# Token gathers of a mixture-of-experts layer: 128 indices each, with the unneeded ones past the table's end

## The chip, the cores and the metric

The kernel runs on one core of a Trainium2 chip. The metric is device time of one execution in microseconds (us), the median of several. Engines are named as in the profile: PE (TensorE matmuls; PEld its weight loads), DVE (VectorE), ACT (ScalarE), POOL (GpSimd), SP (SyncE, which here only issues DMAs). All DMAs, whoever issues them, are carried by 16 DMA engines. Queue q1 of the profile holds the DMAs that SP issues, q0 those that POOL issues.

## The reference

One decoder layer on 512 tokens of width 1024, in float32. What matters here is its last part, the expert layer on `x1` (the tokens after attention and the first normalisation):

```python
logits = (xf @ w_router + b_router)            # 32 experts
top_vals, top_idx = lax.top_k(logits, 4)       # each token goes to 4 experts
gates = softmax(top_vals)
...
xb = x_pad[rows]                               # the rows of one expert's tokens
g = min(xb @ w_gate[e] + b_gate[e], 7)
u = clip(xb @ w_up[e] + b_up[e], -7, 7)
h = g * sigmoid(1.702 * g) * (u + 1)
y = h @ w_down[e] + b_down[e]                  # added to its tokens, times the gate
```

Each expert has three weight matrices of 1024x1024 float32, 4 MiB each, so the 32 experts read 96 matrices. 512 x 4 = 2048 rows go to experts in all.

## The kernel before

Attention, output projection, first normalisation and router take roughly the first 300 us. The expert layer follows, in 32 steps of one expert each. Steps 0, 1 and every odd step up to 29 are *large* (96 token slots), the even steps from 2 to 28 and the last two are *small* (64 slots). Experts are ranked by their number of tokens, so large steps take those with many. With the reference's inputs the router gives these numbers of tokens (counted from the reference's own router):

| steps | tokens in the order of the steps |
|---|---|
| small, 2 to 28 | 64 63 62 62 60 59 59 59 58 57 56 50 50 48 (sum 807) |
| large, 3 to 29 | 89 83 80 73 73 72 70 70 68 67 67 67 67 64 (sum 1010) |
| 0, 1, 30, 31 | 74, 70, 48, 39 |

**Weights.** SP issues them in a fixed order by `wload` (line 669), each matrix as two DMAs of 2 MiB, into a ring of eight 2 MiB tiles with one further tile now and then. An issue waits until PE has finished with the tile that it overwrites.

**Rows of a step.** Two or three steps ahead, `route_info` (or `route_tokens` for step 1) multiplies a one-hot matrix with token numbers on PE, and DVE makes from it `ix` (the token number of each slot, one slot a partition; 0 where a slot has no token) and `gt` (its gate; 0 where a slot has no token). Column 0 holds slots 0 to 63 (twice over the partitions), column 1 slots 64 to 95 (four times). `gather` (line 975) turns `ix` into integers `ii` on 64 partitions, for a large step on 32 more (lines 977 and 979), and POOL issues an indirect DMA (line 981) that reads row `ii[p]` of `x1d` in HBM into partition p of the tile `xg`: 64 or 96 rows of 4 KB. Empty slots fetch row 0. `load_x` (lines 1031 to 1040) then transposes `xg` on PE into `xgA` or `xgB` for the matmuls; there is one buffer of `xg`, so a gather waits until the transposes of the step before have read it. The first step (`gather_early`, line 864) and the last two (`route_pair`, line 1027, 128 rows for two small steps) have gathers of their own.

**Rows back.** `store` (lines 1152 to 1157) computes indices on DVE, and POOL issues indirect DMAs that add the result rows onto `accd` in HBM: one a small step, two a large one, 128 indices each.

**The tile's first user.** Before any of these gathers, the tile `xg` serves as `bds`: `bdown_load` (line 945) has SP read the 32 rows of `b_down` into its first 32 partitions (line 947), and ACT and DVE make `bd3` from it (`bdown_prep`, lines 951 to 953).

Of the kernel before, what the change touches and what calls it, by code (L numbers as in the profile page):

```python
# [9 lines left out]
F32 = mybir.dt.float32  # L10
# [4 lines left out]
ALU = mybir.AluOpType  # L15
# [4 lines left out]
P = 128  # L20
T = 512
NT = T // P
D = 1024
KD = D // P
E = 32
# [20 lines left out]
def _const_array():  # L46
    cols = []

    def put(name, a):
        a = np.asarray(a, np.float32)  # L50
        off = sum(c.shape[1] for c in cols)
        _C[name] = (off, a.shape[1])
        cols.append(a)

    p = np.arange(P)
    put("ident", np.eye(P))
    put("iota", np.tile(np.arange(T)[None, :], (P, 1)))
    ia = (500000.0 ** (-np.arange(0, 32, 2) / 32.0)).astype(np.float32)
    ib = (500000.0 ** (-np.arange(0, 16, 2) / 16.0)).astype(np.float32)
    put("invrow", np.tile(np.concatenate([ia, ib])[None, :], (P, 1)))  # L60
    put("invT", (np.where(p % 32 < 16, -1.0, 1.0) * ia[p % 16])[:, None])
    tb = np.zeros((P, 2 * NT), np.float32)
    tb[:, :NT] = p[:, None]
    tb[:, NT:] = (np.arange(NT) * P)[None, :]
    put("tokid", tb)
    key = (E - 1 - np.arange(E)).astype(np.float32)
    for i in range(NFIX):
        key[i] += 200000.0 + 50000.0 * (NFIX - i)
    put("keyrow", np.tile(key[None, :], (P, 1)))
    put("keycol", key[p % E][:, None])  # L70
    put("eid", (p % E)[:, None])
    seq = np.asarray(RANK_OF_STEP, np.float32)
    sb = np.full((P, 2 * E), -1.0, np.float32)
    sb[96:128, 0:E] = seq
    sb[0:32, E:] = seq
    sb[64:96, E:] = seq
    put("seqblk", sb)
    put("seqrow", np.tile(seq[None, :], (P, 1)))
    put("iodup", np.tile(np.concatenate([np.arange(64)] * 2 + [np.arange(64, 96)] * 4)[None, :], (P, 1)))
    pad = np.stack([T + p % 64, T + 64 + p % 32], 1)  # L80
    put("padrow", pad)
    put("padidx", np.stack([2 * pad[:, 0] + p // 64, 4 * pad[:, 1] + p // 32], 1))
    put("rowmul", np.tile(np.array([[2.0, 4.0]]), (P, 1)))
    put("j64", np.tile((64.0 * np.arange(8))[None, :], (P, 1)))
    return np.ascontiguousarray(np.concatenate(cols, 1))


CONST = _const_array()


# [12 lines left out]
def kernel(ctx: ExitStack, tc: tile.TileContext, a: dict, out: bass.AP, dbg=None):  # L103
    nc = tc.nc
    dbg = dbg or {}
    V, S, G, PE = nc.vector, nc.scalar, nc.gpsimd, nc.tensor
# [9 lines left out]
    x1d = dr.tile([T, D], F32, name="x1d")  # L116
# [21 lines left out]
    def C(name):  # L138
        o, n = _C[name]
        return cst[:, o:o + n]  # L140
# [34 lines left out]
    def bank(name):  # L175
        return pp.tile([P, 512], F32, tag="b", name=name)
# [765 lines left out]
    p3 = ctx.enter_context(tc.tile_pool(name="p3", bufs=1))  # L942
    xgB = p3.tile([P, KD, 96], F32, name="xgB")
    bd3 = p3.tile([96, D], F32R, name="bd3")
    def bdown_load():
        b = p3.tile([P, D], F32, tag="xg", name="bds")[0:E]
        nc.sync.dma_start(b, a["b_down"])
        return b

# [12 lines left out]
    def route_tiles(n):  # L962
        xs = p3.tile([P, 2, 8], F32, tag="xs", name=f"xs{n}", bufs=3)
        ix = p3.tile([P, 2], F32, tag="ix", name=f"ix{n}", bufs=4)
        gt = p3.tile([P, 2], F32, tag="gt", name=f"gt{n}", bufs=4)
        ii = p3.tile([P, 1], I32, tag="ii", name=f"ii{n}", bufs=3)
        return xs, ix, gt, ii

    def route_mm(px, oh, rhs_t, large, lo, hi):
        for c in range(2 if large else 1):  # L970
            for t in range(NT):
                PE.matmul(px[:, 8 * c + lo:8 * c + hi], oh[:, t, 128 * c:128 * c + 128], rhs_t(t),
                          start=(t == 0), stop=(t == NT - 1))

    def gather(n, ii, ix, large):
        Cn = 96 if large else 64
        V.tensor_copy(ii[0:64], ix[0:64, 0:1])  # L977
        if large:
            V.tensor_copy(ii[64:96], ix[64:96, 1:2])
        xg = p3.tile([P, D], F32, tag="xg", name=f"xg{n}")  # L980
        G.indirect_dma_start(out=xg[0:Cn], out_offset=None, in_=x1d,  # L981
                             in_offset=bass.IndirectOffsetOnAxis(ap=ii[0:Cn], axis=0))
        return xg

    def route_info(n, oh, rhs_t, large):
        px = ps_tr(f"px{n}").rearrange("p a b -> p (a b)")
        route_mm(px, oh, rhs_t, large, 0, 5)
        nx = 2 if large else 1
        xs, ix, gt, ii = route_tiles(n)
        V.tensor_copy(xs[:, 0:nx, 0:5], px[:, 0:16].rearrange("p (a b) -> p a b", a=2)[:, 0:nx, 0:5])  # L990
        V.tensor_tensor(ix[:, 0:nx], xs[:, 0:nx, 0], xs[:, 0:nx, 1], ALU.add)
        V.tensor_reduce(gt[:, 0:nx], xs[:, 0:nx, 2:5], AX.X, ALU.add)
        return ii, ix, gt

    def route_tokens(n, oh):
        px = bank(f"pxt{n}")
        route_mm(px, oh, lambda t: RT[:, t, 0:2, n], True, 0, 2)
        xs, ix, gt, ii = route_tiles(n)
        V.tensor_copy(xs[:, :, 0:2], px[:, 0:16].rearrange("p (a b) -> p a b", a=2)[:, :, 0:2])
        V.tensor_tensor(ix, xs[:, :, 0], xs[:, :, 1], ALU.add)  # L1000
        return xs, gather(n, ii, ix, True), ix, gt

    def route_gates(n, oh, xs, xg, ix, gt):
        px = bank(f"pxw{n}")
# [4 lines left out]

    def route(n, oh, rhs_t, large):  # L1010
        ii, ix, gt = route_info(n, oh, rhs_t, large)
        return gather(n, ii, ix, large), ix, gt

    def route_pair(n, oh):
        px = bank(f"px{n}")
# [181 lines left out]
    def overflow(nv):  # L1197
# [45 lines left out]
        with tc.For_i(0, nv, 1) as i:  # L1243
# [15 lines left out]
            V.tensor_tensor(gr_, gr_, rt[:, :, 3], ALU.subtract)  # L1259
            V.tensor_copy(rt[:, :, 4], gr_)  # L1260
            xg, ix, gt = route(100, route_oh(100, row[:, 0:NT].unsqueeze(2), False), lambda t: rt[:, t, :], False)
            xt = load_x(100, xg, False)
            pg_ = ps_gu("ovpg")
# [40 lines left out]
    def rstep(s, oh):  # L1304
        return route(s, oh, lambda t: RT[:, t, :, s], LARGE[s])

    bds = bdown_load()

    scr = xgB.rearrange("p a b -> p (a b)")
# [301 lines left out]
    mat64(pu_, xgA, st0.wu, sel0, b3[:, 1, :], ks=range(1, 2))  # L1611
    bdown_prep(bds)
    rt1 = route_tokens(1, oh1)
    g, sg = swi_g1(0, pg0, 512)
    prep_counts()
# [97 lines left out]
```

## Time and profile before

| | |
|---|---|
| three runs | 1352.81, 1354.06, 1355.06 us; median 1354.06 us |
| the profiled execution | 1354.38 us, of which the span from first to last instruction is 1352.6 us |
| busy in the span | PE 92%, DVE 29%, ACT 19%, POOL 13% |
| moved by DMA | 454.28 MB; q1 428.15 MB, q0 24.78 MB |

Shares of busy time are averages over the whole span. The DMA share of a stretch is the time that its packets took, over 16 engines and the stretch's length; packets of one engine can overlap, so it can be a little over 1. The chain of waits follows, from the last instruction back, what released each piece of work; a "DMA" piece in it lasts from the DMA's issue to its landing, the time in the DMA queue included.

### The profile page before, as it was taken

The page shows a single profiled execution, that of the slowest core. Times are in us where ns is not written, and L with a number is a line of the kernel's source. Part 1 is how long each engine was busy: PE and PEld are TensorE (multiplying, and loading weights), DVE is VectorE, ACT ScalarE, POOL GpSimd, SP SyncE. Part 2 cuts the span into 40 slices and gives each one's busy share as a digit, 9 for nine tenths or more (in the row PEclk, how much of TensorE's full clock was granted, in tenths as well). Part 3 has the DMA queues.
Part 4 walks back from the last instruction along what each step waited for, and adds up shares of the span by engine and source line. Part 5 has one row for each costly group of instructions (what it writes and reads, how often), then busy time and mean ns, then how long its engine had stood idle before and what let it go on. Part 6 is the DMA issues. An engine that isn't in the chain of part 4 may idle for free.

```text
span 1352.6 us, 20619 instructions
## 1 busy us (share of the span) xinstructions
PE 1240.9 (92%) x8596; PEld 577.6 (43%) x8596; DVE 392.3 (29%) x1020; ACT 262.7 (19%) x588; POOL 179.0 (13%) x184
## 2 busy tenths in 40 slices
PE   9999998898999999898989898989797989899985
PEld 8887555443344343333333333333333333333331
DVE  6765667453121211111111111111111111111125
ACT  5544655231101111011101010101010101010113
POOL 0540221001011011011010101010101010100013
PEclk9999999898999999999999999999999999899978
DMA  8031064489999999999999999999999999999992
GB/s 312 0 125 63 7 256 171 172 333 358 380 390 401 394 381 403 395 401 394 403 396 402 394 399 399 398 398 400 397 398 396 402 394 401 397 420 409 420 377 97
DMA packets 45824, 454.28 MB, mean 336 GB/s; under 512 B 5856, under 2 KB 8672, under 8 KB 20256
## 3 DMA queue, kind: packets, MB, share of 16 engines
q1 hardware_dynamic: 34848, 428.15, 78.3%
q0 software_dynamic: 10880, 24.78, 7.4%
q8 instruction: 69, 1.13, 0.3%
q14 instruction: 27, 0.22, 0.0%
HBM read 436.39 MB, written 16.52 MB: 335 GB/s over the span
## 4 chain that ended last, share of the span: by engine, by line
PE 57%; DMA 38%; DVE 2%; issue 1%; ACT 0%; SPq 0%; POOL 0%; POOLq 0%; DVEq 0%; ACTq 0%
DMA wu<-w_up 33%; PE pu L624 10%; PE pg L624 9%; PE pd L624 9%; PE puz L634 3%; PE mx L556 3%; DMA wd<-w_down 3%; PE pd L1046 2%; PE pj L200 2%; PE pj L201 2%; PE pj L202 2%; PE pxg L1039 1%; DMA xg<-x1d,ii 1%; PE sc L469 1%; PE av L510 1%; PE pgz L634 1%
## 5 line engine op out<-in xcount | busy, mean ns | idle before, releaser
L624 PE MATMUL pd<-wd,hT 128*64 128x512 f32 x1024 | 231.2, 602 | 14.1 <-DMA wd<-w_down 14.1
L1157 POOL DMA_INDIRECT accd<-y,si x46 | 73.5, 1598 | 534.4 <-ACT y L1162 356.6
L624 PEld LDWEIGHTS pd<-wd,hT 128*64 128x64 f32 x1024 | 73.5, 138 | 158.2 <-issue 138.6
L624 PE MATMUL pg<-wg,xgB 128*64 128x512 f32 x512 | 123.4, 626 | 17.2 <-DMA wg<-w_gate 17.2
L624 PE MATMUL pu<-wu,xgB 128*64 128x512 f32 x512 | 118.9, 618 | 0.0
L624 PE MATMUL pg<-wg,xgA 128*64 128x512 f32 x512 | 117.9, 600 | 0.0
L624 PE MATMUL pu<-wu,xgA 128*64 128x512 f32 x512 | 114.6, 596 | 1.8 <-DMA wu<-w_up 1.8
L1062 DVE TENSOR_SCALAR u<-pu 128x512 f32<-128x512 f32 x31 | 21.4, 691 | 324.6 <-PE pu L628 324.5
L634 PE MATMUL puz<-wu,xgB 128*32 128x256 f32 x960 | 70.7, 447 | 46.2 <-DMA wu<-w_up 46.2
L624 PEld LDWEIGHTS pg<-wg,xgB 128*64 128x64 f32 x512 | 38.6, 142 | 88.9 <-issue 87.0
L981 POOL DMA_INDIRECT xg<-x1d,ii x29 | 27.3, 941 | 350.5 <-DVE ii L977 232.7
L634 PEld LDWEIGHTS puz<-wu,xgB 128*32 128x32 f32 x960 | 34.2, 124 | 85.6 <-DMA wu<-w_up 38.3
L1040 ACT COPY xgB<-pxg 128x384 f32<-128x384 f32 (+1 forms) x32 | 14.6, 472 | 286.0 <-PE pxg L1039 285.9
L624 PEld LDWEIGHTS pu<-wu,xgB 128*64 128x64 f32 x512 | 36.5, 143 | 75.1 <-issue 74.5
L624 PEld LDWEIGHTS pu<-wu,xgA 128*64 128x64 f32 x512 | 34.9, 137 | 73.1 <-issue 66.9
L624 PEld LDWEIGHTS pg<-wg,xgA 128*64 128x64 f32 x512 | 34.8, 137 | 61.1 <-issue 59.5
L1062 DVE TENSOR_SCALAR uz<-puz 128x256 f32<-128x256 f32 x16 | 6.8, 424 | 185.5 <-PE puz L638 185.5
L1046 PE MATMUL pd<-wd,hT 128*32 128x256 f32 x1024 | 58.8, 381 | 0.0
L634 PE MATMUL pgz<-wg,xgB 128*32 128x256 f32 x960 | 57.1, 391 | 0.0
L1162 ACT ACTIVATE y<-pd,gt 128x512 f32<-128x512 f32 x30 | 20.6, 687 | 170.3 <-PE pd L624 170.3
L1052 DVE TENSOR_SCALAR g<-pg 128x512 f32<-128x512 f32 x32 | 22.1, 691 | 89.0 <-PE pg L628 89.0
L1040 ACT COPY xgA<-pxg 128x256 f32<-128x256 f32 x30 | 11.2, 372 | 189.2 <-PE pxg L1039 188.2
(447 smaller groups left out, 1517.3 us busy)
## 6 DMA issues: line engine op xcount, KB each, us to landing
wg<-w_gate SPq DMA_DIRECT2D x64, 2048.0 KB, 40.0
wu<-w_up SPq DMA_DIRECT2D x64, 2048.0 KB, 40.0
wd<-w_down SPq DMA_DIRECT2D x62, 2048.0 KB, 40.1
wd<-w_down SPq DMA_DIRECT2D x3, 1024.0 KB, 33.0
hat<-wB SPq DMA_DIRECT2D x1, 2048.0 KB, 12.8
hwk<-wB SPq DMA_DIRECT2D x1, 2048.0 KB, 17.0
hwv<-wB SPq DMA_DIRECT2D x1, 2048.0 KB, 7.2
hwk<-w_o SPq DMA_DIRECT2D x1, 2048.0 KB, 7.3
```

Of the source, the lines that this page charges most:

```text
L200: PE.matmul(o, xh[:, k, tt], h[:, 0:n], start=(k == 0), stop=False)
L201: PE.matmul(o, xh[:, k, tt], l[:, 0:n], start=False, stop=False)
L202: PE.matmul(o, xl[:, k, tt], h[:, 0:n], start=False, stop=(k == KD - 1))
L556: PE.matmul(ps[h], attnT[:, k, t * P:(t + 1) * P], wo[k // 4][:, k % 4, hs], start=(k == 0), stop=(k == KD - 1))
L624: PE.matmul(ps[64 * c:64 * c + 64, :], xt[:, k, 0:64], w[k // 4][:, k % 4, hf * 512:(hf + 1) * 512], start=(st and k == 0), stop=(k == KD ...
L634: PE.matmul(o[32 * c:32 * c + 32, :], xt[:, k, 64:96], w[k // 4][:, k % 4, c * 256:(c + 1) * 256], start=(k == 0), stop=False)
L981: G.indirect_dma_start(out=xg[0:Cn], out_offset=None, in_=x1d, in_offset=bass.IndirectOffsetOnAxis(ap=ii[0:Cn], axis=0))
L1040: S.copy(xgT[:, 4 * h:4 * h + 4, 0:Cn], pt[:, :, 0:Cn])
L1046: PE.matmul(ps[32 * c:32 * c + 32, 0:256], ht[:, k, :], wd[k // 4][:, k % 4, c * 256:(c + 1) * 256], start=(k == 0), stop=(k == KD - 1))
L1052: V.tensor_scalar(g, pgt, 7.0, None, ALU.min)
L1062: V.tensor_scalar(u, pup, 7.0, -7.0, ALU.min, ALU.max)
L1157: G.indirect_dma_start(out=dst, out_offset=bass.IndirectOffsetOnAxis(ap=si[:, i:i + 1], axis=0), in_=self.y[:, lo:hi], in_offset=None, com ...
```

## The change

Every gather that goes through `gather` (steps 1 to 29, and the overflow path that doesn't run with these inputs) now has 128 indices. To an index that isn't wanted 2048 is added, which puts it past the 512 rows of `x1d`, and the indirect DMA gets a bound of 511 with the instruction to pass over indices beyond it. Unwanted are, by a new constant `dup`, the partitions that repeat other slots (64 to 127 in a small step, 96 to 127 in a large one), and, where `gt` is already known, the slots whose gate is 0 (`sk`). In step 1 the gates come later, so only the repeats are left out there. Partitions that are passed over keep what `xg` held; so that this is a number from the start, POOL clears all of `bds` before `b_down` is loaded.

```diff
+    put("dup", 4.0 * T * np.stack([p >= 96, p >= 64], 1))
...
     def bdown_load():
-        b = p3.tile([P, D], F32, tag="xg", name="bds")[0:E]
+        b = p3.tile([P, D], F32, tag="xg", name="bds")
+        G.memset(b, 0.0)
+        b = b[0:E]
         nc.sync.dma_start(b, a["b_down"])
...
-    def gather(n, ii, ix, large):
-        Cn = 96 if large else 64
-        V.tensor_copy(ii[0:64], ix[0:64, 0:1])
+    def gather(n, ii, ix, gt, large):
+        sk = p3.tile([P, 2], F32, tag="sk", name=f"sk{n}", bufs=2)
+        xg = p3.tile([P, D], F32, tag="xg", name=f"xg{n}")
+        if gt is not None:
+            w = slice(0, 2 if large else 1)
+            V.tensor_scalar(sk[:, w], gt[:, w], 0.0, 4.0 * T, ALU.is_le, ALU.mult)
+            V.tensor_tensor(sk[:, w], sk[:, w], ix[:, w], ALU.add)
+        else:
+            sk = ix
+        dup = C("dup")
         if large:
-            V.tensor_copy(ii[64:96], ix[64:96, 1:2])
-        xg = p3.tile([P, D], F32, tag="xg", name=f"xg{n}")
-        G.indirect_dma_start(out=xg[0:Cn], out_offset=None, in_=x1d,
-                             in_offset=bass.IndirectOffsetOnAxis(ap=ii[0:Cn], axis=0))
+            V.tensor_tensor(ii[0:64], sk[0:64, 0:1], dup[0:64, 0:1], ALU.add)
+            V.tensor_tensor(ii[64:P], sk[64:P, 1:2], dup[64:P, 0:1], ALU.add)
+        else:
+            V.tensor_tensor(ii, sk[:, 0:1], dup[:, 1:2], ALU.add)
+        G.indirect_dma_start(out=xg, out_offset=None, in_=x1d,
+                             in_offset=bass.IndirectOffsetOnAxis(ap=ii, axis=0), bounds_check=T - 1, oob_is_err=False)
         return xg
```

POOL's instructions from the last store of the attention part to the first result rows (`accd`), the kernel before:

```order
L753 DMA accd<-acc 128x1024
L981 DMA xg_2700<-x1d,ii_2695 96x1024
L981 DMA xg_2940<-x1d,ii_2935 64x1024
L1157 DMA accd<-y_2958,si_2962 1216x512
L1157 DMA accd<-y_2958,si_2962 2432x256
L981 DMA xg_3035<-x1d,ii_3029 96x1024
```

and with the change:

```order
L754 DMA accd<-acc 128x1024
L948 MEMSET bds 128x1024
L993 DMA xg_2700<-x1d,ii_2696 128x1024
L993 DMA xg_2944<-x1d,ii_2939 128x1024
L1169 DMA accd<-y_2967,si_2971 1216x512
L1169 DMA accd<-y_2967,si_2971 2432x256
L993 DMA xg_3043<-x1d,ii_3038 128x1024
```

One clearing of 128x1024 stands ahead of the first gather, every gather has 128 rows to fill, and nothing else moves on POOL. SP's list is the same as before; its load of `bds` now waits for POOL.

DVE's instructions that make the indices of step 2 (small), behind the routing matmul `px` of that step, and the store's indices of step 0 behind them, the kernel before:

```order
L990 COPY xs_2932<-px_2927 128x5
L991 TENSOR_TENSOR ix_2933<-xs_2932 128x1
L992 TENSOR_REDUCE gt_2934<-xs_2932 128x1
L977 CAST ii_2935<-ix_2933 64x1
L1152 TENSOR_TENSOR sx_2961<-ix_2871,cst 128x2
L1153 SCALAR_TENSOR_TENSOR sx_2961<-gt_2872,sx_2961 128x2
L1154 TENSOR_TENSOR sx_2961<-sx_2961,cst 128x2
L1155 TENSOR_TENSOR si_2962<-sx_2961,cst 128x2
```

and with the change:

```order
L1002 COPY xs_2936<-px_2931 128x5
L1003 TENSOR_TENSOR ix_2937<-xs_2936 128x1
L1004 TENSOR_REDUCE gt_2938<-xs_2936 128x1
L983 TENSOR_SCALAR sk_2943<-gt_2938 128x1
L984 TENSOR_TENSOR sk_2943<-sk_2943,ix_2937 128x1
L992 TENSOR_TENSOR ii_2939<-sk_2943,cst 128x1
L1164 TENSOR_TENSOR sx_2970<-ix_2875,cst 128x2
L1165 SCALAR_TENSOR_TENSOR sx_2970<-gt_2876,sx_2970 128x2
L1166 TENSOR_TENSOR sx_2970<-sx_2970,cst 128x2
L1167 TENSOR_TENSOR si_2971<-sx_2970,cst 128x2
```

Three small instructions stand where one cast stood; in a large step four where two stood. In all 58 more on DVE.

## Rows read from the trace of the kernel before

**Rows 1.** Three stretches of the span; busy us of each engine, then clock, DMA share, GB/s.

```profile
core 0: us, PE busy (x) PEld busy (x) DVE busy (x) ACT busy (x) POOL busy (x), PEclk, DMA share, GB/s
285.00:290.00 5.00, 5.00 (x74) 2.36 (x72) 3.90 (x12) 3.37 (x3) 0.00 (x0) 0.87 0.31 85
...
325.00:350.00 25.00, 25.00 (x220) 10.65 (x220) 5.76 (x14) 1.79 (x4) 2.52 (x2) 0.89 0.89 325
350.00:1290.00 940.00, 862.62 (x6312) 347.88 (x6310) 158.88 (x437) 96.31 (x190) 96.20 (x72) 0.97 1.02 399
```

**Rows 2.** Chain of waits around one pair of steps: start us, us, what.

```profile
607.56 37.84 DMA wu<-w_up
...
673.87 39.19 DMA wu<-w_up
...
741.83 37.69 DMA wu<-w_up
```

**Rows 3.** DMA queues from 350 to 1290 us: packets, MB, share of 16 engines.

```profile
q1 hardware_dynamic: 24436, 355.87, 92.6%
q0 software_dynamic: 8847, 18.50, 8.6%
```

**Rows 4.** The same view from 666.7 to 671 us, one small step's gather.

```profile
q1 hardware_dynamic: 77, 1.13, 86.5%
q0 software_dynamic: 72, 0.26, 19.2%
```

**Rows 5.** The same view from 695.7 to 701.9 us, one large step's gather.

```profile
q1 hardware_dynamic: 123, 1.77, 85.4%
q0 software_dynamic: 112, 0.39, 19.6%
```

**Rows 6.** Chain of waits where step 2's rows are fetched: start us, us, what.

```profile
313.31 1.06 PE pxg L1039 x8
...
315.53 0.17 DVE si L1155
...
315.80 9.01 DMA xg<-x1d,ii
324.80 0.14 issue
324.94 1.11 PE pxg L1039 x8
```

**Rows 7.** Timeline, POOL then PE: a small step's gather and the transposes that use it.

```profile
662.64 0.94 POOL L981 DMA_INDIRECT xg<-x1d,ii  x1 [20.78 <-DVE ii L977]
...
688.23 1.09 PE L1039 MATMUL pxg<-cst,xg 64*128 64x64 f32 x8
```

**Rows 8.** All uses of xg: time of its gathers from issue to landing.

```profile
DMA to landing us min/median/max: 6.3/10.4/14.4
```

**Rows 9.** Timeline around the load of b_down: SP, ACT, DVE.

```profile
283.65 0.33 SPq L947 DMA_DIRECT2D bds<-b_down  x1
287.62 2.06 SPq L669 DMA_DIRECT2D wu<-w_up  x2
...
286.06 1.04 ACT L951 CAST bd<-bds 32x1024 fp32r<-32x1024 f32 x1 [2.44 <-issue]
...
292.18 0.63 ACT L1053 ACTIVATE sg<-g 128x512 f32<-128x512 f32 x1 [2.70 <-DVE g L1052]
...
290.73 0.16 DVE L999 COPY xs<-pxt 128x4 f32<-128x4 f32 x1 [1.40 <-PE pxt L972]
```

**Rows 10.** Groups of instructions on POOL that are nearest to the new clearing.

```profile
L411 POOL COPY hk<-hk 32x3584 f32<-32x3584 f32 x1 | 3.2, 3171 | 10.2 <-ACT hk L410 10.2
L376 POOL COPY kro<-kro 128x384 f32<-128x384 f32 x1 | 0.8, 849 | 0.1
```

**Rows 11.** Groups on DVE by tile: duration ns min/median/max, first and last start us, forms.

```profile
L977 DVE CAST ii<-ix x29: 145/146/147, 291.1 to 1160.6; 64x1 int32<-64x1 f32 x29
...
L1152 DVE TENSOR_TENSOR sx<-ix,cst x30: 142/152/155, 315.0 to 1267.0; 128x2 f32<-128x2 f32 x16, 128x1 f32<-128x1 f32 x14
```

More of the change, by code (lines that the diff above doesn't have):

```diff
@@ L1000, in route_tokens @@
         V.tensor_tensor(ix, xs[:, :, 0], xs[:, :, 1], ALU.add)
-        return xs, gather(n, ii, ix, True), ix, gt
+        return xs, gather(n, ii, ix, None, True), ix, gt
     def route_gates(n, oh, xs, xg, ix, gt):
@@ L1011, in route @@
         ii, ix, gt = route_info(n, oh, rhs_t, large)
-        return gather(n, ii, ix, large), ix, gt
+        return gather(n, ii, ix, gt, large), ix, gt
     def route_pair(n, oh):
```

## The prediction, made before the changed kernel was run

> **What bounds the kernel now.** I read the stretches first. From 350 to 1290 us, in 940 of the 1352.6 us of the span, the DMA share is 1.02 at 399 GB/s, while PE is busy 862.6 us of the 940 and DVE 158.9 [rows 1]. So the sixteen DMA engines have no time left there, and everyone else has some. The chain of waits says the same: about every 67 us, the time of two steps, it falls back into a load of w_up that takes 38 to 39 us from issue to landing, nearly all of it spent in the queue behind other loads [rows 2]. What counts in this stretch is therefore the time that each DMA engine needs for its packets. Weights take 92.6% of it and POOL's queue 8.6%, gathers and the adding of result rows together [rows 3]. A PE wait, a DVE instruction or a later landing costs nothing here as long as the next load can still be issued.
>
> Before 350 us it is different. From 325 to 350 the share is 0.89 [rows 1], because PE had stood still for 9.0 us, waiting for the rows of step 2 [rows 6], and so freed weight tiles late.
>
> **Price of a gathered row.** While 64 rows of 4 KB go through, POOL's queue takes 19.2% of 16 engines for 4.3 us, 13.2 us of engine time [rows 4]; 96 rows take 19.6% of 6.2 us, 19.4 us [rows 5]. That is 0.206 and 0.202 us a row. I take 0.205. Below lies the price of as many bytes of weights: 92.6% of 940 us on 16 engines is 13,927 us for 355.87 MB, or 0.160 us per 4096 bytes. Above lies the mean of all POOL's transfers: 8.6% for 18.50 MB, 0.286 us per 4096 bytes [rows 3]. The rows' own price is measured on the operation itself, so I choose it and keep the others for the range.
>
> **How rows lie on the engines.** A weight packet takes 0.57 us on average (13,927 us for 24,436 packets [rows 3]). An engine that alternates a row with a weight packet needs 0.78 us a turn. On sixteen engines 64 rows are four turns, 3.1 us, and 96 rows six, 4.7 us; on eight engines they would be 6.2 and 9.3 us. Seen are at most 4.3 and 6.2 us [rows 4, 5]. So today all sixteen share each gather evenly, four rows each in a small step, six in a large one, ten for a pair of steps.
>
> **What the change removes.** In the 14 small and 14 large steps from 2 to 29, 14 x 160 = 2240 rows are fetched now, and 807 + 1010 = 1817 belong to a token. 423 rows fall away, 1.73 MB. Spread over all sixteen engines that is 423 / 16 x 0.205 = 5.4 us. Steps 1, 30 and 31 save nothing.
>
> **What it does to the balance.** The list is now 128 long, and its wanted entries aren't spread over it: entries 0 to 63 hold up to 64 tokens, 64 to 95 the few beyond 64 (0 to 25 in a large step), the rest nothing. If a list of any length is cut into sixteen runs, four entries long at 64 and six at 96, it is eight at 128, and entries 0 to 63 fall to eight engines. Six of these carry 8 rows in every small step (none has under 48 tokens) and 8 in every large one (none has under 64): 16 rows a pair where they had 10. The weights of each load are still shared by all sixteen, and a tile is full when the last engine is done, so the busiest engines set the pace. Six more rows at 0.205 us are 1.23 us a pair. Thirteen pairs fetch their rows after 350 us: **+16.0 us**. If entries are dealt out in turn instead, every engine gets four or fewer, and the gain above remains. [Rows 4, 5] fit both, since they show full lists only. I lean to the runs, 50 against 35, as the plainer way to divide a transfer among engines.
>
> [...]
>
> **Step 2's rows.** In the same case its 64 rows are eight turns of one engine instead of four, 3.1 us later by the turn above, 4.3 by [rows 4]. PE waits for exactly this landing [rows 6]. A wait of 9.0 us cost the DMA engines 0.13 x 25 = 3.3 us afterwards [rows 1], 0.36 us per us; so I take **+1.5 us**, between 1.1 and, if every us counts, 4.3. Steps 2 and 3 lie ahead of 350 and are paid with this term. Later gathers have room: issued at 662.64, used at 688.23, 25.6 us [rows 7], against a slowest landing of 14.4 us [rows 8].
>
> **More on DVE.** Each gather's indices need two instructions more, about 0.15 us each [rows 11], 58 in all. DVE is busy 17% of the stretch [rows 1], and the 25.6 us of [rows 7] cover 0.3 us. Without that cover, in step 2, they come ahead of `si`, behind which the gather starts [rows 6]: 0.3 x 0.36, **+0.1 us** (0 to 0.3).
>
> **The clearing.** POOL's copies take 3.17 us for 3584 elements and 0.85 for 384 [rows 10], so 1024 elements cost 0.9 to 2.3 us; I take 1.5, between them. SP's load of `bds` at 283.65 moves to 284.6 to 286.0. Behind it on SP wait the loads of w_up, but these are held until 287.62 anyway [rows 9], and on POOL the gather of step 1 comes after 292 us. ACT's casts of `bds` move along, covered by the 2.70 us that ACT stands idle before `sg`; DVE has 1.40 us before `xs` [rows 9], so 0 to 0.9 us of it show. I take **+0.2 us**. If the clearing took over 4 us, it would hold the loads of w_up while the DMA engines are at a share of 0.31 [rows 1], us for us.
>
> Passing over an entry may cost POOL time in making its list; no row shows it, and 25.6 us cover it except in step 2, where it is bounded by nothing and one more issue's 0.94 us [rows 7].
>
> **Sum.** 1354.4 (this execution; the runs' median is 1354.06) + 16.0 + 1.5 + 0.1 + 0.2 = **1372.2 us**, 1.3% slower. With the bounds of the price and of step 2 this case reaches from 1354.4 + 12.5 + 1.1 = 1368 to 1354.4 + 22.3 + 4.3 + 1.2 = 1382. If the engines relieved are by chance those that lag today, which no row tells, it is less, down to about 1362.
>
> **Rivals.**
> - *Dealt in turn, faster* (35%). The engine that is dealt first holds the tokens divided by 16, rounded up: 14 rows fewer in all than now, 2.9 us; the mean is 5.4. The same 0.3 us for clearing and indices come on top: 1349.3 to 1351.8, likely 1350.5. For it: today's rows are perfectly even. It decides if the wanted rows of a small step still pass in about 4.3 us.
> - *Nothing is passed over* (5%). Should an index past the end be held at the last row instead, each gather moves 128 rows, eight on every engine: 16 a pair against 10, the same +16 us by another way, about 1372. The test is POOL's bytes: 5.6 MB more instead of 1.7 fewer.
> - *Little shows* (10%). The runs may be shorter than eight entries, or rows on one half may let weight packets on it go faster; gain and loss then nearly cancel, at 1352 to 1358.
>
> **Chances.** A measurement of this kernel can tell about 0.2%, 2.7 us, from no change. The first case and the unpassed rows make slower 0.55. Of the dealt case, whose 2.6 to 5.1 us lie across that mark, I count 0.24 as faster and 0.11 as the same; of the last 0.04 and 0.06. Together 0.28, 0.17, 0.55. The range must hold both signs: from 1349 to 1379, leaving out the far ends of the dealt case and of the price. The likeliest case's own range is 1362 to 1382.
>
> **What the profile will show.** Right: POOL's queue moves about 23.05 MB instead of 24.78; the rate from 350 us on falls from 399 to some 390 GB/s and the DMA share with it, below 1.02, since half of the engines wait at each load; a small step's rows pass in 6 to 9 us instead of 4.3 and the median landing grows from 10.4 us by about 3; step 2's wait grows from 9.0 to about 12.5. Wrong, if the share stays at 1.02 and rows pass as quickly as now (dealt), or if POOL's bytes grow (not passed over). The clearing is wrong if the w_up loads after `bds` start later than 287.62 by more than 0.5 us.

## The result, and the profile after

The changed kernel takes 1330.86 us (median of four runs, 1330.19 to 1331.53) against 1354.56 us of the kernel before beside it: a ratio of 0.9825, with 95% interval 0.9808 to 0.9842. It is 1.75% faster. The forecast was 1372.2 us, 1.3% slower, and its range began at 1349: wrong in sign and by 41 us. The profiled execution of the changed kernel took 1330.19 us, its span 1328.3.

The page of the changed kernel: busy time, two of the rows by slices of the span (33 us each), and the queues.

```profile
span 1328.3 us, 20706 instructions
PE 1226.0 (92%) x8596; PEld 574.1 (43%) x8596; DVE 402.4 (30%) x1076; ACT 262.6 (20%) x588; POOL 183.4 (14%) x185
...
DMA  8031074478999999999999999999999999999972
GB/s 318 0 128 64 1 266 157 185 286 348 359 393 412 409 420 413 412 419 413 421 413 418 414 417 414 419 415 417 413 415 412 414 416 407 413 410 413 382 296 85
...
q1 hardware_dynamic: 34848, 428.15, 77.3%
q0 software_dynamic: 12256, 23.05, 7.0%
```

POOL's queue moves 23.05 MB, exactly the 1.73 MB less that 423 rows of 4 KB are. The weights are the same 428.15 MB. The stretches that answer to [rows 1]:

```profile
core 0: us, PE busy (x) PEld busy (x) DVE busy (x) ACT busy (x) POOL busy (x), PEclk, DMA share, GB/s
285.00:290.00 5.00, 5.00 (x72) 2.38 (x64) 3.71 (x11) 2.75 (x3) 0.00 (x0) 0.82 0.41 98
325.00:350.00 25.00, 21.76 (x202) 9.68 (x204) 4.13 (x13) 1.79 (x4) 2.61 (x2) 0.81 0.71 241
350.00:1267.00 917.00, 851.04 (x6330) 345.56 (x6326) 170.46 (x492) 96.33 (x190) 99.23 (x72) 0.99 1.01 412
```

From 350 us on the DMA engines are as full as before (1.01 against 1.02) and carry 412 GB/s instead of 399. So the gain is not work that has gone: each byte takes the engines less time. Ahead of 350 the kernel has become worse: a share of 0.71 instead of 0.89.

Which bytes became cheaper is seen where a gather passes. The queues of the changed kernel from 660.5 to 666.4 us, a small step's gather with 59 tokens, and then from 689.7 to 695.1, a large one with 70:

```profile
q1 hardware_dynamic: 157, 2.29, 91.5%
q0 software_dynamic: 140, 0.24, 10.8%
...
q1 hardware_dynamic: 139, 2.02, 87.1%
q0 software_dynamic: 136, 0.29, 13.6%
```

Engine time a MB of weights is the share times the stretch times 16 over the MB. Here it is 0.915 x 5.9 x 16 / 2.29 = 37.7 and 37.3 us. In the kernel before it was 0.865 x 4.3 x 16 / 1.13 = 52.7 us beside a list of 64 [rows 4] and 47.9 beside one of 96 [rows 5], while the whole stretch had 39.1 [rows 3]. Against 37.7 that is 17.0 and 18.1 us of engine time for each gather, 1.06 and 1.13 us on each of sixteen engines; 14 of each kind make 30.7 us. That is where the time came from: **while a list of 64 or 96 rows passed, the weight packets beside it took 27 to 40% more engine time, and this has gone.** The rows themselves fell from 0.206 us to 10.2 / 59 = 0.17, the packets of passed-over entries included.

The 30.7 us rest on one gather of each kind. The whole stretch bears them out. The weights' queue of the changed kernel from 350 to 1250 us:

```profile
q1 hardware_dynamic: 24389, 355.30, 93.1%
```

That is 0.931 x 900 x 16 / 355.30 = 37.7 us a MB, the price beside a gather, against 39.1 before [rows 3]: 1.4 us a MB less for some 356 MB are 31 us on each of sixteen engines.

The trace of the kernel before already held a list of 128, the gather for the last two steps (line 1027). Its issue, and the queues from 1204.6 to 1210.6 us while its rows pass:

```profile
1200.51 1.02 POOL L1027 DMA_INDIRECT xg<-x1d,ii  x1 [3.76 <-DVE ii L1025]
```

```profile
q1 hardware_dynamic: 139, 2.02, 79.3%
q0 software_dynamic: 136, 0.52, 21.5%
```

20.6 us of engine time for 128 rows, 0.161 us each, and weights at 37.7 us a MB. Had these two rows been put beside [rows 4, 5], the gain would have been in the sum.

The new instructions, on POOL and then SP (the timeline of the changed kernel), and what PE waited for between 300 and 345 us, first in the changed kernel, then in the one before:

```profile
283.75 0.95 POOL L948 MEMSET bds<- 128x1024 f32 x1 [7.45 <-ACT pg L785]
...
284.73 0.33 SPq L950 DMA_DIRECT2D bds<-b_down  x1
287.69 2.05 SPq L670 DMA_DIRECT2D wu<-w_up  x2
```

```profile
PE pxg L1051 <- DMA xg<-x1d,ii: 7.7, 1, 7.7
```

```profile
PE pxg L1039 <- DMA xg<-x1d,ii: 4.5, 1, 4.5
```

The clearing takes 0.95 us, and the w_up loads behind it start 0.07 us later than before: nothing. The wait for the rows of step 2 grew by 3.2 us.

### The profile page after: what moved, and what is told of

Read it like the earlier page. It is cut to its first block, busy times and chain, and to the rows that moved or that the text cites. A ratio compares the mean times of both kernels' runs of the same rounds, so it can differ in the third digit from the quotient of the medians.

```text
span 1328.3 us, 20706 instructions
## 1 busy us (share of the span) xinstructions
PE 1226.0 (92%) x8596; PEld 574.1 (43%) x8596; DVE 402.4 (30%) x1076; ACT 262.6 (20%) x588; POOL 183.4 (14%) x185
## 3 DMA queue, kind: packets, MB, share of 16 engines
q1 hardware_dynamic: 34848, 428.15, 77.3%
q0 software_dynamic: 12256, 23.05, 7.0%
q8 instruction: 69, 1.13, 0.3%
## 5 line engine op out<-in xcount | busy, mean ns | idle before, releaser
L625 PE MATMUL pd<-wd,hT 128*64 128x512 f32 x1024 | 228.4, 596 | 9.4 <-DMA wd<-w_down 9.3
L625 PE MATMUL pu<-wu,xgB 128*64 128x512 f32 x512 | 115.7, 605 | 0.0
L635 PE MATMUL puz<-wu,xgB 128*32 128x256 f32 x960 | 62.3, 406 | 44.2 <-DMA wu<-w_up 44.1
L993 POOL DMA_INDIRECT xg<-x1d,ii x29 | 30.5, 1053 | 342.8 <-DVE ii L992 250.5
L1174 ACT ACTIVATE y<-pd,gt 128x512 f32<-128x512 f32 x30 | 20.6, 687 | 162.2 <-PE pd L625 162.2
```

The costliest lines, as they stand in the source:

```text
L625: PE.matmul(ps[64 * c:64 * c + 64, :], xt[:, k, 0:64], w[k // 4][:, k % 4, hf * 512:(hf + 1) * 512], start=(st and k == 0), stop=(k == KD ...
L635: PE.matmul(o[32 * c:32 * c + 32, :], xt[:, k, 64:96], w[k // 4][:, k % 4, c * 256:(c + 1) * 256], start=(k == 0), stop=False)
L993: G.indirect_dma_start(out=xg, out_offset=None, in_=x1d, in_offset=bass.IndirectOffsetOnAxis(ap=ii, axis=0), bounds_check=T - 1, oob_is_er ...
L1174: S.activation(st.y[:, 0:512], pd, AF.Copy, scale=st.gt[:, 0:1])
```

## The experiments

Two things could make the change fast. *Theory A*: a list of 128 is itself better than one of 64 or 96. *Theory B*: fewer rows are fetched (or row 0 no longer many times at once). Three kernels, on one chip, tell them apart; those after them test the balance and the cause.

**A list of 128 with nothing passed over**, an edit of the kernel before:

```diff
         V.tensor_copy(ii[0:64], ix[0:64, 0:1])
-        if large:
-            V.tensor_copy(ii[64:96], ix[64:96, 1:2])
+        V.tensor_copy(ii[64:P], ix[64:P, c:c + 1])      # c is 1 in a large step
...
-        G.indirect_dma_start(out=xg[0:Cn], ..., ap=ii[0:Cn], ...
+        G.indirect_dma_start(out=xg, ..., ap=ii, ...
```

> The kernel before with 128 indices in every gather and nothing passed over: repeats and empty slots are all fetched, 3712 rows in steps 1 to 29 instead of 2336. Theory A (what counts is that the list is 128 long, so that a row takes 0.16 us instead of 0.203 and the weight packets beside it 0.61 us instead of 0.78): all engines carry 8 rows a gather, as many as the busiest do in the changed kernel, so about the time of the changed kernel, 1328 to 1336 us. Theory B (what counts is that rows are no longer fetched): 16 rows a pair instead of 10 at 0.2 us, so 1365 to 1385 us.

Measured: 1334.09 us, ratio 0.9852 (0.9834 to 0.9870), though it fetches 7.4 MB more than the changed kernel. The queues from 597.6 to 603.9 us, one gather:

```profile
q1 hardware_dynamic: 153, 2.20, 82.2%
q0 software_dynamic: 144, 0.52, 20.5%
```

Weights at 37.7 us a MB, rows at 20.7 / 128 = 0.16 us. So theory B fails for the greater part: 20 of the 24 us come without a row fewer. What it is about the longer list that helps is tested further below. Shared evenly, an estimate, the 256 rows of a pair are 16 on each of sixteen engines here; if eight carry as many in the changed kernel, and the busiest set the pace, the two should take about the same time, and they lie 3.2 us apart.

**Empty slots passed over, lists of 64 and 96**, an edit of the changed kernel:

```diff
+        Cn = 96 if large else 64
+        V.tensor_copy(ii[0:64], sk[0:64, 0:1])
...
+            V.tensor_copy(ii[64:96], sk[64:96, 1:2])
...
-        G.indirect_dma_start(out=xg, ..., ap=ii, ...
+        G.indirect_dma_start(out=xg[0:Cn], ..., ap=ii[0:Cn], ...
```

> The changed kernel with lists of 64 and 96 again, empty slots still passed over: 1817 rows in steps 2 to 29, like the changed kernel. Theory A: rows still take about 0.2 us and weight packets beside them 0.78 us; with lists cut into runs the first engines keep 4 and 6 rows, so 1346 to 1355 us. Theory B (fewer rows, or no more repeats of row 0): about the changed kernel's 1331 us.

Measured: 1350.92 us, ratio 0.9976 (0.9966 to 0.9985). The queues from 603.3 to 607.9 us, a small step with 59 tokens:

```profile
q1 hardware_dynamic: 86, 1.25, 88.2%
q0 software_dynamic: 76, 0.24, 17.8%
```

Weights at 0.882 x 4.6 x 16 / 1.25 = 51.9 us a MB, rows at 0.22 us: as slow as before. Passing over the empty slots is worth 3.4 us by itself (1354.35 before, beside it), and repeats of row 0 aren't the cause.

**A list of 128 in the large steps alone**, the small ones with 64 (`Cn = P if large else 64` in the changed kernel):

> The changed kernel with 128 indices in the large steps alone, the small ones with 64 and empty slots passed over. Theory A: the slowing of weight packets goes with the rows fetched by short lists, 6 turns an engine in a large step and 4 in a small one, so about 60% of the gain remains, 1337 to 1343 us, and rows take 0.16 us in large steps and 0.2 us in small ones. If only lists that don't divide into a power of two (96) are slow: about 1331 us. If only short ones (64) are: about 1350 us.

Measured: 1337.60 us, ratio 0.9872 (0.9853 to 0.9892). The queues of one kernel beside a list of 64 (596.8 to 601.2 us) and then beside one of 128 (629.1 to 635):

```profile
q1 hardware_dynamic: 83, 1.20, 87.3%
q0 software_dynamic: 75, 0.24, 17.0%
...
q1 hardware_dynamic: 155, 2.26, 89.5%
q0 software_dynamic: 142, 0.30, 12.8%
```

51.2 and 37.4 us a MB, in the same run. The slowing comes and goes with the list beside which the weights pass. And both kinds of short list are slow: longer large lists alone bring 13.3 of the 20.1 us between the kernel with short lists and the changed one.

**The rows spread**, an edit of the changed kernel, is an attempt to bring them onto all sixteen engines. This tests the part of the prediction that is left, the balance:

```diff
+        V.tensor_copy(ii, C("far"))                     # 2048 everywhere
+        V.tensor_copy(ii[0:32], sk[0:32, 0:1])
+        V.tensor_copy(ii[64:96], sk[32:64, 0:1])
+        if large:
+            V.tensor_copy(ii[32:64], sk[64:96, 1:2])
...
+                    PE.transpose(pt[:, j, 0:96], xv[0:96, 4 * h + j, :], ident[0:96, 0:96])
+                S.copy(xgT[:, hs, 0:64]...,  pt...[:, :, :, 0:32])     # columns 0-31 and 64-95
+                if large:
+                    S.copy(xgT[:, hs, 64:96], pt[:, :, 32:64])
```

> The changed kernel with the wanted entries laid out otherwise: slots 0 to 31 on partitions 0 to 31, 32 to 63 on 64 to 95, 64 to 95 of a large step on 32 to 63, the rest past the end; the transposes take 96 rows and ACT puts the columns in order. [...] If each engine serves eight neighbouring partitions, eight engines still carry 8 rows in a small step: 5 to 6 us a gather and about 1331 us.

Measured: 1317.11 us (1317.05 to 1319.36), ratio 0.9726 (0.9709 to 0.9744), 13.8 us less than the changed kernel. The queues from 593.8 to 597 us, a small step's gather:

```profile
q1 hardware_dynamic: 72, 1.13, 82.6%
q0 software_dynamic: 70, 0.24, 18.6%
```

59 rows pass in 3.2 us instead of 5.9. With 0.16 us a row and 0.61 a weight packet (16 KB at 37.4 us a MB), four turns of an engine that takes one of each are 3.1 us and eight are 6.2, an estimate. So the two times fit entries 0 to 31 and 64 to 95 on all sixteen engines, and entries 0 to 63 on eight, though not as eight neighbouring entries each: then this layout would again have filled only eight engines. That is inferred from the times; no row names the engine that serves a partition.

The imbalance that the prediction feared shows in these times (5.9 against 3.2 us), but not in the rate. From 350 to 1250 us the spread layout carries as much as the changed kernel (355.30 MB of weights, above):

```profile
q1 hardware_dynamic: 24383, 355.18, 93.0%
```

What differs is when a whole tile has come and been used, and with it SP's next issue. One w_down load early in the stretch and the first half of the last w_up, in the changed kernel and then with the rows spread:

```profile
350.38 3.99 SPq L670 DMA_DIRECT2D wd<-w_down  x2
...
1241.90 0.33 SPq L1303 DMA_DIRECT2D wu<-w_up  x1
```

```profile
352.21 3.99 SPq L670 DMA_DIRECT2D wd<-w_down  x2
...
1229.30 0.33 SPq L1312 DMA_DIRECT2D wu<-w_up  x1
```

The spread layout is 1.8 us behind at the first and 12.6 us ahead at the second, 14.4 us gained on the way. The likely reading is that in the changed kernel the eight relieved engines work ahead on loads that are already queued, and the tile still waits for the other eight; no row names the engines, so this is argued.

**Why short lists are slow.** In the kernel before, a list of 64 passed in 4.3 us. Four turns of a row at 0.206 us and a weight packet at 0.86 (16 KB at 52.7 us a MB) are 4.3 us, so by this estimate all sixteen engines shared it, while entries 0 to 63 of a list of 128 fit eight. Suppose that the weight loads divide the partitions among the engines as a list of 128 does. Then, of the sixteen engines that share a list of 64 from partition 0, eight write partitions that the other eight serve. From partition 32 on, half of the list falls on partitions 32 to 63 and half on 64 to 95, and every engine can have partitions of its own. That is *theory P*, a conjecture, since no row names the engines; *theory L* is that short lists are slow as such. Two kernels differ in nothing but the offset, on top of the spread layout for large steps:

```diff
+        if not large:
+            V.tensor_copy(ii[0:64], sk[0:64, 0:1])
+            G.indirect_dma_start(out=xg[32:96], ..., ap=ii[0:64], ...)     # the other: xg[0:64]
+            return xg
...
+                if not large:
+                    S.copy(xgT[:, hs, 0:64], pt[:, :, 32:96])              # the other: 0:64
+                    continue
```

> As the spread layout, but a small step's list has 64 indices and is written to partitions 32 to 95. Theory P (an engine slows others when it writes partitions that another engine serves in the weight loads: a list of 64 gives each engine four neighbouring rows, and from partition 32 on these are its own): rows at 0.16 us, weight packets beside them at 0.61 us, time as the spread layout, 1315 to 1321 us. Theory L (short lists are slow as such): rows at 0.2 us and weight packets beside small gathers at 0.78 us, 1325 to 1333 us.

> The same kernel with the list of 64 written to partitions 0 to 63, as in the kernel before; it differs from the one written to partitions 32 to 95 in nothing else. Theory P: half of the engines write partitions that the other half serve, so rows at 0.2 us, weight packets beside them at 0.75 to 0.8 us, 1325 to 1333 us. Theory L: the same time as from partition 32. If neither matters in the spread layout: 1317 us for both.

Measured: **1314.40 us** from partition 32 (1313.75 to 1316.31, ratio 0.9713, 0.9699 to 0.9726), 1329.47 us from partition 0 (1328.33 to 1331.14, ratio 0.9818, 0.9805 to 0.9831). The queues while a small step's 59 rows pass, from partition 32 (588.1 to 591.1 us) and from partition 0 (596.9 to 601.2 us):

```profile
q1 hardware_dynamic: 67, 1.05, 81.6%
q0 software_dynamic: 66, 0.24, 19.7%
```

```profile
q1 hardware_dynamic: 76, 1.08, 81.7%
q0 software_dynamic: 74, 0.24, 19.1%
```

37.3 against 52.0 us a MB of weights, 0.16 against 0.22 us a row, by the place alone. Theory L has fallen, and with it theory A in its words: a list of 64 from partition 32 is as good as one of 128 (37.3 us a MB beside it, 37.4 beside the spread layout's). Nor is it partitions 0 to 63 as such, whoever writes them: in the changed kernel the 59 rows go to the same partitions out of a list of 128, in 5.9 us instead of 4.3, and the weights beside them stay at 37.7 us a MB. Of the two theories P is left for lists of 64, still a conjecture: no row names the engine, and by what way one would slow another is open. Why a list of 96 is slow too (47.9 us a MB beside it [rows 5]) no run shows.

From partition 32 the time is 0.6 us below its range and 2.7 us below the spread layout's. PE's wait for the rows of step 2 is 5.1 us there and 6.6 with the spread layout; where the rest comes from is open.

**The extra rows of large steps by turns** on partitions 32 to 63 and 96 to 127, an edit of the spread layout. If these two stretches of partitions lie on different engines, as theory P supposes, the extra rows of two large steps are shared by both halves of the engines:

> [...] If the busiest engine sets the pace: 2 rows a pair fewer on it at 0.16 us, 4 to 5 us in 14 pairs, 1311 to 1315 us. If the balance no longer matters at this level (slots 64 to 95 are mostly empty): 1316 to 1319 us.

Measured: 1317.13 us (1316.95 to 1317.80), ratio 0.9731 (0.9717 to 0.9744), the spread layout's time, in the second range: the few tokens beyond 64 no longer set the pace there, or the engines are divided otherwise than supposed; which one is open. So the gain of the spread layout can't be put down to the fullest engine alone. The kernel from partition 32 is the fastest, 2.9% below the kernel before and 1.2% below the changed one.

## Why the prediction was wrong

- **What bounds the kernel: right.** From 350 to 1250 us the share is 1.01 or 1.02 in all nine kernels.
- **Price of a gathered row: the step that failed.** It read q0's line alone. "The rows' own price is measured on the operation itself, so I choose it" took 0.205 us as all that a row costs, and "How rows lie on the engines" gave the weight packet beside it the average 0.57 us. The q1 lines of the same rows say otherwise: 52.7 and 47.9 us a MB against 39.1. So did its own turns: 64 rows should have passed in 3.1 us and took 4.3, 96 in 4.7 and took 6.2. It read these only as "at most", as a sign that sixteen engines share the rows; the 1.2 and 1.5 us left over are mostly the slowed weights (1.06 and 1.13). A gather's full cost in the kernel before was 2.05 us of rows a pair and 2.2 us of slowed weights, and the second term, 30.7 us in all, is missing from the sum. No rival had it at its size. "Little shows" let weight packets go faster on the half without rows, enough to cancel the loss; the lowest time of any rival was 1349.3.
- **What the change removes: right.** 423 rows, 1.73 MB, to the digit; that they are really passed over was given 95%. Alone they bring 3.4 us, near the 2.9 that were worked out for the fullest engine, though by another way of cutting the list, so the nearness is luck in part.
- **What it does to the balance: the mechanism right in the main, the term about right.** The times fit entries 0 to 63 on eight engines: 59 rows take 5.9 us in the changed kernel and 3.2 with the rows spread; no row names the engines. The way to it was wrong in part: with an engine's eight entries in one run, the spread layout would have filled eight engines again, some 6.2 us by the estimate above. The sum had +16.0 us for six rows a pair. By the same reading the spread layout leaves 8 to 12 of the 16 rows on an engine, and it brought 13.8 us; four to eight rows in 14 pairs at 0.16 are 9 to 18 us, an estimate. The price fell to 0.16 with the change, so six rows were nearer 14 x 6 x 0.16 = 13.4 us than 16.0. And half of the engines "wait at each load" by no row: the share stayed at 1.01, and the loss shows in the issues.
- **Step 2: right in direction, too small.** The 9.0 us for which PE "had stood still" were the time from issue to landing; PE stood idle for 4.5 us of it and 7.7 now. The share from 325 to 350 fell from 0.89 to 0.71, 4.5 us of DMA time where +1.5 was taken, just over the bound of 4.3. Some of the added wait isn't balance: with the rows spread it was still 6.6 us and with lists of 64 and 96 passed over 6.1.
- **DVE and clearing: right.** Step 2's gather was issued at 316.33 us instead of 315.80, 0.5 us later where 0.3 was given. The clearing took 0.95 us of the 0.9 to 2.3 allowed, `bds` started at 284.73 as given, w_up at 287.69 (was 287.62).
- **The sum again**, with the term that was missing and the others as measured: 1354.4 - 30.7 + 13.4 - 14 x 10 x 0.045 (ten rows a pair, 0.205 to 0.16) + 4.5 = 1335, against 1330.2. This is an estimate made afterwards: it counts the first pair's rows twice (in 13.4 and in 4.5), and some 5 us stay unexplained. With the slowed weights in it the prediction's own sum would have come out on the right side.

The signs that the prediction gave for being right were half there: fewer bytes and slower passing of a small gather came, the rate went up to 412 GB/s instead of down to 390. Rows that pass more slowly at a higher rate point to the weights. A share that stays at 1.02 was to mean entries dealt in turn; it stayed at 1.01 while 59 rows took 5.9 us, not the 4.3 of the dealt case, so the share tells nothing of the balance here.

## What to carry to other kernels

When a transfer shares full DMA engines with another stream, price it by what both queues took in the window where it passes, not by its own packets: divide share by bytes for each, and compare with a window without it. In these runs the length of a list and its first partition decided what it cost the 128-partition loads beside it: beside 128 entries, or 64 from partition 32, they took 37.3 to 37.7 us a MB, and beside 64 from partition 0 51.2 to 52.7; with no gather beside them, in the kernel before from 660 to 666 us, it was 1.021 x 6 x 16 / 2.62 = 37.4. If theory P is right, what helped is that each engine kept to the partitions that it serves in the steady stream; that remains a conjecture. Then try where the live entries lie: on partitions 0 to 31 and 64 to 95 instead of 0 to 63 they brought 13.8 us here. Look for a lack of balance in the times of the loads' issues: bytes and share of all engines together hid it here (355.30 and 355.18 MB, 1.01 in both). And look for the same operation in another shape in the trace that is already there.

## What the runs showed that was not expected

- A shift of 32 partitions takes a 4 KB row from 0.16 to 0.22 us and the weights beside it from 37.3 to 52.0 us a MB. Theory P would put it down to engines that write partitions of others; no row names the engines.
- An entry that is passed over still leaves a packet. Steps 1 to 29 have 29 x 128 - 2336 = 1376 entries more than before, and q0 has 12256 - 10880 = 1376 packets more, though 1.73 MB less. Packets under 512 bytes rose by 1799, these 1376 and the 423 of empty slots, as the DMA lines of the two pages say, before and after:

```profile
DMA packets 45824, 454.28 MB, mean 336 GB/s; under 512 B 5856, under 2 KB 8672, under 8 KB 20256
```

```profile
DMA packets 47200, 452.55 MB, mean 341 GB/s; under 512 B 7655, under 2 KB 10471, under 8 KB 21632
```
